# Left-operand sums of the down projection formed once and kept in DRAM, the sample tile first in the output projection, the gate in the accumulation, output rows in two parts

## The chip, the cores and the metric

The kernel runs on one core of a Trainium2 chip. The metric is device time in microseconds (us) of one execution. The engines are named as the profile names them: PE (matrix products; PEld is its weight load), DVE (the vector engine), ACT (the scalar engine), POOL (GpSimd) and SP, whose queue issues every DMA of this kernel in order.

## The reference

One layer of a hybrid encoder for 2048 prompt frames and 32 sample frames, width 1024, in float32. Cut to what matters here:

```
proj = (rmsnorm(x, ln1_g) * (1 + sc1) + sh1) @ w_in       # q, k, v for attention, u for the state-space layer
attn = sliding_window_attention(q, k, v)                  # 512 columns
ssm  = gelu_and_glu(state_space(u))                       # 512 columns
x    = x + g1 * (concat(rmsnorm(attn), rmsnorm(ssm)) @ w_out)
h2   = rmsnorm(x, ln2_g) * (1 + sc2) + sh2
ff   = (silu(h2 @ w_gate) * (h2 @ w_up)) @ w_down         # 1024 -> 2816 -> 1024
y    = x + g2 * ff
```

The modulation vectors sh1, sc1, g1, sh2, sc2, g2 come from the conditioning vector, one set for the prompt and one for the sample.

## The kernel before, in words

There are four stages. Stage A projects the 16 prompt tiles of 128 frames and the sample tile (number 16, `NPT`) and writes q, k, v and u to DRAM. Stage B runs the state-space layer with part of the attention. Stage C runs the rest of the attention, the GLU (`c_prep`, units in the order `UNITS`), the norms (`c_norm`) and the output projection (`c_out`), the last two tile by tile in the order `TILES`: 8 to 15, 0 to 7, then the sample tile. Stage F is the feed-forward part. The stages overlap: each is written as Python generators ("flows") that are advanced in turn, and a scheduler at compile time orders the instructions of each engine by the program's order, letting later ones pass when earlier ones aren't ready in its own simulation. On the chip each engine's order is then fixed.

Every product is made from two float32r parts of each operand: `split` (L111) copies the high part on ACT and subtracts it on DVE for the low part, and three matmuls (high by high, high by low, low by high) are accumulated.

**Stage F** works on three panels of frames (`PIECES`, 704, 704 and 672 columns; half of a panel, `w`, is 352, 352 and 336). In a panel, layer 0 multiplies by `w_gate` and `w_up` (11 units of 256 columns each), and layers 1 to 3 multiply by row blocks of `w_down` (2 units each; 1024, 1024 and 768 rows). A unit is a Strassen-Winograd scheme: seven products (`PRODUCTS`, L68, p = 0 to 6) in place of eight, each for two weight blocks (m = 0, 1), so 24 matmuls of `w` columns for each m and k group of four, and 18 in layer 3. One product is called a step. The left operands are the weight quarters 11, 12, 21, 22 and four sums of them, s1 to s4. The right operands are the four quarters of the panel and four sums, t1 to t4.

- `start_unit` (L1526), called one unit ahead, loads four half blocks [128, 4, 256] through `weights` (six buffers `wr`).
- `prepare` (L1531), called three steps ahead (`AHEAD`), forms the sums on POOL in place: s1 and s3 at p = 0, s2 at p = 1, s4 at p = 2, 128x512 elements each, for both m, and then splits the operand of its step (`wh` on ACT, `wl` on DVE). This happens in all four layers and in all three panels, so that the sums of `w_down`, which are the same each time, are formed three times.
- `prepare_right` (L1560), six steps ahead and in the first unit of a layer only, splits the seven right operands (`bh`, `bl`, 128x1408) and forms t1 to t4 with four subtractions on DVE (`q`).
- `finish` (L1648) takes the results from PSUM. In layer 0 it makes silu(gate) * up (`finish_in`), whose last product runs on POOL, and stores it to `f_d`. In layers 1 to 3 `finish_out` (L1631) adds to the accumulators `acc`, with part of the additions on POOL (`c<-c,acc`).
- `out_rows` (L1585) is started after the last product of each half of layer 3: it multiplies the four accumulators by g2 on ACT, and for each of six pieces loads the rows of x (`xr`, three buffers), transposes (`fo`), adds on DVE and stores.
- `h_steps` (L1419) makes the next panel's right operand while layer 3 runs (transposes `ft`).

Of the kernel before, what the change touches and what calls it, by code (L numbers as in the profile page):

```python
# [50 lines left out]
LATE = [0, 1, 2, 3, 4, 5]  # L51
TILES = [*range(8, NPT), *range(8), NPT]
UNITS = [4, 5, 6, 7, 0, 1, 2, 3, 8]
BLOCKS = [2, 0, 1, 3]
PSB = 5
# [17 lines left out]
def hybrid_kernel(  # L73
# [1021 lines left out]
    def attention_tile(j):  # L1095
# [21 lines left out]
        if j < NPT:  # L1117
            vcur = kv_split(kf, vf, kt[:, :, 128:256], n)
            if j == TILES[0]:
# [163 lines left out]
    def c_prep(u):  # L1283
# [39 lines left out]
        ssm[u] = (mh, ml, ss)  # L1323
        if h:
            g_load({2: 3, 3: 0, 0: 1, 1: 4}[b])
        yield 1
# [34 lines left out]
    def c_out(j):  # L1361
# [5 lines left out]
        c0 = 128 * (j % 2)  # L1367
        if j in (TILES[0], NPT):
            g1b[0] = pcw.tile([128, D], F32, tag="g1b", name="g1b", bufs=1)[0:n]
            SP.dma_start(g1b[0], gr_d[s:s + 1].to_broadcast([n, D]))  # L1370
# [48 lines left out]
    def h_steps(sb):  # L1419
# [3 lines left out]
        for grp in (PIECES[sb][0:3], PIECES[sb][3:6]):  # L1423
# [23 lines left out]
            col = c  # L1447

    cg = wo_steps(range(4, 8), stage, 512)
    fp = Flow(c_prep, 9, 1, 0)  # L1450
# [38 lines left out]

    class Layer:  # L1490
        def __init__(self, sb, i):
            self.sb, self.i, self.w = sb, i, HALF[sb]
            self.kt = 3 if i == 3 else 4
            self.units = KF // 2 if i == 0 else 2

        def weights(self, u, m):

            kt = self.kt
            out = []
            for h in range(2):  # L1500
                r = pwr.tile([128, 4, 256], F32, tag="wr", name="wr", bufs=6)[:, 0:kt]
                if self.i == 0:
                    src = (w_gate, w_up)[m][0, h * 512:(h + 1) * 512, u * 256:(u + 1) * 256]
                else:
                    row = (self.i - 1) * 1024 + h * kt * 128
                    src = w_down[0, row:row + kt * 128, (2 * u + m) * 256:(2 * u + m + 1) * 256]
                SP.dma_start(r, src.rearrange("(k p) n -> p k n", p=128))
                out.append(r)
            return out

        def load(self):

            q = quads(self.kt)
            qd[self.sb, self.i] = q
            for a in range(2):
                m = 8 * (self.i - 1) + a * self.kt
                for b in range(2):
                    SP.dma_start(q[a][b][:, :, 0:self.w],
                                 f_d[self.sb][m:m + self.kt, :, b * self.w:(b + 1) * self.w].rearrange("k p n -> p k n"))

    layers = [Layer(sb, i) for sb in range(3) for i in range(4)]
    steps = [(L, u, p) for L in layers for u in range(L.units) for p in range(7)]
    raw, left, right = {}, {}, {}
    acc = {}

    def start_unit(n):  # L1526
        if n < len(steps):
            L, u, _ = steps[n]
            raw[L, u] = [L.weights(u, m) for m in range(2)]

    def prepare(n):  # L1531

        if n >= len(steps):
            return
        L, u, p = steps[n]
        kt, w = L.kt, L.w
        an, bn, _ = PRODUCTS[p]
        qs = []
        for m in range(2):
            r0, r1 = raw[L, u][m][0:2]  # L1540
            a11, a21, a12, a22 = r0[:, :, 0:128], r0[:, :, 128:256], r1[:, :, 0:128], r1[:, :, 128:256]
            if p == 0:
                s1 = pwr.tile([128, 4, 128], F32, tag="s1", name="s1", bufs=2)[:, 0:kt]
                raw[L, u][m].append(s1)
                tt(P, s1, a21, a22, ADD)
                tt(P, a21, a11, a21, SUB)
            elif p == 1:
                tt(P, a11, raw[L, u][m][2], a11, SUB)
            elif p == 2:
                tt(P, a12, a12, a11, SUB)  # L1550
            qs.append({"11": a11, "12": a12, "22": a22, "s1": raw[L, u][m][2], "s2": a11, "s3": a21, "s4": a12}[an])
        left[n] = []
        for m in range(2):
            h, l = (pv.tile([128, 4, 128], F32R, tag="wv", name=nm, bufs=4 * AHEAD + 4)[:, 0:kt] for nm in ("wh", "wl"))
            split(h, l, qs[m], A, V)
            left[n].append((h, l))
        if u == L.units - 1 and p == 6:
            raw.pop((L, u))

    def prepare_right(n):  # L1560
# [24 lines left out]
    def out_rows(L, half):  # L1585

        sb = L.sb
        ns = sum(n for j, _, n in PIECES[sb] if j < NPT)
# [5 lines left out]
        col = 0  # L1594
        tiles = [acc.pop(d) for d in range(4 * half, 4 * half + 4)]
        for j, r0, n in PIECES[sb]:
            hs_ = slice(half * 512, (half + 1) * 512)
            row = j * 128 + r0
            xr = pwr.tile([128, 512], F32, tag="xr", name="xr", bufs=3)[0:n]
            SP.dma_start(xr, x1_d[row:row + n, hs_])  # L1600
            pb = fp_["t"].tile([128, 512], F32, tag="ft", name="fo")[0:n]
# [3 lines left out]
            SP.dma_start((y_sample[0] if j >= NPT else y_prompt[0, row:row + n])[:, hs_], xr)  # L1605
            col += n
            yield 1
# [23 lines left out]
    def finish_out(L, u, m, qd_, c, bank):  # L1631
        w = L.w
        i, j = qd_
        d = 4 * u + 2 * m + i
        if L.i == 1 and d not in acc:
            acc[d] = pv.tile([128, 2 * HW], F32, tag=f"acc{d}", name="acc")
        o = acc[d][:, j * w:(j + 1) * w]
        if c is None:
            if L.i == 1:
                act(o, bank)  # L1640
            else:
                tt(V, o, bank, o, ADD)
        else:
            if L.i > 1:
                tt(P, c, c, o, ADD)
            tt(V, o, bank, c, ADD)

    def finish(n):  # L1648
        L, u, p = steps[n]
        w = L.w  # L1650
        for m in range(2):
            x, y, z = (banks.get((t, m)) for t in "xyz")
            if p in (0, 2, 4):
                c = keep()[:, 0:w]
                act(c, x[:, 0:w])
                cs[m, p] = c
            if p in (1, 4, 5, 6):
# [7 lines left out]
    start_unit(0)  # L1665
    for n in range(6):
        if n < AHEAD:
            prepare(n)
        prepare_right(n)
    coming = []  # L1670
    for n, (L, u, p) in enumerate(steps):
        li = layers.index(L)
# [81 lines left out]
```

## Time and profile before

| | |
|---|---|
| three runs | 2426.49, 2432.91, 2432.59 us; median 2432.59 |
| the profiled execution's own time | 2427.46 us |
| its span, first to last instruction | 2425.6 us |
| mean granted TensorE clock | 0.961 |
| DVE, ACT, POOL busy, share of the span | 73%, 52%, 58% |
| stage F, from about 954 us on | 1472 us |

A row of the view of windows gives, for a stretch of the span, the busy time and the count of instructions of each engine, the granted clock and the share of the DMA engines. A row of a group gives the line, the engine, what is written from what, the shape, the count, and then busy time and mean. The chain of waits gives start, duration and what ran, along the chain of work that ended last. Names such as `wl`, `bl`, `q` are the program's tile names.

### The profile page before, as it was taken

What the parts mean: (1) busy time and instruction counts of PE and PEld (TensorE: products, weight loads), DVE (VectorE), ACT (ScalarE), POOL (GpSimd) and SP (SyncE); (2) the same over time, 40 slices, a digit from 0 to 9 for tenths busy, and PEclk for the clock granted to TensorE, in tenths of its full rate; (3) what the DMA queues carried; (4) which work ended last, traced back from release to release, by engine and by line L of the source; (5) the groups of instructions that cost most, each with busy time, mean ns of one, the idle gap of its engine ahead of it and who ended that gap; (6) DMA issues with size and microseconds to landing.
All of it is one profiled execution on the core that took longest, in us unless ns stands there. A gap on an engine that the chain in (4) does not pass through costs nothing.

```text
span 2425.6 us, 38219 instructions
## 1 busy us (share of the span) xinstructions
PE 2238.5 (92%) x13262; PEld 2068.3 (85%) x13262; DVE 1769.5 (73%) x2722; ACT 1264.8 (52%) x2557; POOL 1418.6 (58%) x1277
## 2 busy tenths in 40 slices
PE   7888998997998898899999999999999989999987
PEld 4677777886887786799999888999989889999887
DVE  6878876778687754855568988655589896667995
ACT  5645435546555555444445575444455754445543
POOL 1177766784655645655555665655556646555563
PEclk8898998998999999899999999999999999999999
DMA  7757767764221223333324335333243254332322
GB/s 232 263 174 211 229 204 230 226 212 156 83 74 56 69 76 132 112 125 124 110 99 130 97 122 185 119 124 111 98 129 97 81 171 144 124 127 96 124 91 92
DMA packets 291455, 331.03 MB, mean 136 GB/s; under 512 B 50798, under 2 KB 237258, under 8 KB 291260
## 3 DMA queue, kind: packets, MB, share of 16 engines
q1 hardware_dynamic: 291260, 328.58, 43.2%
q8 instruction: 104, 1.70, 0.3%
q14 instruction: 91, 0.75, 0.1%
HBM read 247.14 MB, written 81.37 MB: 135 GB/s over the span
## 4 chain that ended last, share of the span: by engine, by line
PE 58%; DVE 11%; DMA 5%; POOL 4%; issue 4%; ACT 3%; SPq 0%; DVEq 0%; ACTq 0%; POOLq 0%
PE fx L116 25%; PE fy L116 12%; PE fz L116 6%; PE co L116 4%; DVE wl L88 3%; DVE bl L88 2%; PE cb L116 2%; PE ob L116 1%; DVE q L88 1%; PE y L116 1%; DMA wr<-in_w_down_dram 1%; POOL wr L88 1%; PE qp L116 1%; PE pt L1067 1%; DMA out_dram<-xr 1%
## 5 line engine op out<-in xcount | busy, mean ns | idle before, releaser
L88 DVE TENSOR_TENSOR wl<-wr,wh 128x512 fp32r<-128x512 f32 (+1 forms) x612 | 567.9, 941 | 253.3 <-ACT wh L100 240.3
L100 ACT ACTIVATE wh<-wr 128x512 fp32r<-128x512 f32 (+1 forms) x612 | 374.7, 617 | 550.0 <-PE fx L116 298.1
L116 PE MATMUL fx<-bh,wh 128*128 128x352 f32 (+1 forms) x1584 | 514.4, 325 | 16.5 <-ACT wh L100 7.1
L116 PE MATMUL fx<-bl,wh 128*128 128x352 f32 (+1 forms) x1584 | 512.3, 323 | 9.5 <-DVE bl L88 9.5
L116 PE MATMUL fx<-bh,wl 128*128 128x352 f32 (+1 forms) x1584 | 513.6, 324 | 1.8 <-DVE wl L88 1.8
L88 POOL TENSOR_TENSOR s<-wr 128x512 f32<-128x512 f32 (+1 forms) x102 | 145.4, 1426 | 365.4 <-DVE wl L88 180.6
L88 POOL TENSOR_TENSOR wr<-wr 128x512 f32<-128x512 f32 (+1 forms) x204 | 325.7, 1599 | 43.7 <-DVE wl L88 38.8
L116 PEld LDWEIGHTS fx<-bh,wh 128*128 128x128 f32 x1584 | 302.3, 191 | 19.9 <-ACT wh L100 8.0
L116 PEld LDWEIGHTS fx<-bl,wh 128*128 128x128 f32 x1584 | 303.1, 191 | 10.3 <-DVE bl L88 10.3
L116 PEld LDWEIGHTS fx<-bh,wl 128*128 128x128 f32 x1584 | 301.8, 191 | 3.0 <-DVE wl L88 2.7
L116 PE MATMUL fy<-bh,wh 128*128 128x352 f32 (+1 forms) x792 | 256.2, 324 | 15.1 <-DVE acc L88 13.1
L116 PE MATMUL fy<-bh,wl 128*128 128x352 f32 (+1 forms) x792 | 254.6, 322 | 2.3 <-DVE wl L88 2.3
L116 PE MATMUL fy<-bl,wh 128*128 128x352 f32 (+1 forms) x792 | 254.4, 321 | 0.0
L88 POOL TENSOR_TENSOR wr<-s,wr 128x512 f32<-128x512 f32 (+1 forms) x102 | 152.2, 1500 | 83.0 <-DVE wl L88 82.9
L88 POOL TENSOR_TENSOR c<-c 128x352 f32<-128x352 f32 (+1 forms) x99 | 136.5, 1378 | 83.7 <-ACT wh L100 56.4
L88 DVE TENSOR_TENSOR bl<-q,bh 128x1408 fp32r<-128x1408 f32 (+3 forms) x84 | 164.0, 1957 | 5.3 <-ACT bh L100 5.2
L116 PEld LDWEIGHTS fy<-bh,wh 128*128 128x128 f32 x792 | 150.0, 189 | 19.7 <-DVE acc L88 16.5
L100 ACT ACTIVATE c<-fx 128x352 f32<-128x352 f32 (+1 forms) x339 | 150.3, 444 | 4.9 <-PE fx L116 4.8
L116 PEld LDWEIGHTS fy<-bh,wl 128*128 128x128 f32 x792 | 149.0, 188 | 3.2 <-DVE wl L88 3.2
L116 PEld LDWEIGHTS fy<-bl,wh 128*128 128x128 f32 x792 | 149.9, 189 | 0.0
L116 PE MATMUL fz<-bh,wh 128*128 128x352 f32 (+1 forms) x396 | 129.1, 326 | 15.0 <-ACT wh L100 15.0
L100 ACT ACTIVATE bh<-q 128x1408 fp32r<-128x1408 f32 (+3 forms) x84 | 107.4, 1284 | 65.1 <-DVE q L88 64.8
(386 smaller groups left out, 5435.9 us busy)
## 6 DMA issues: line engine op xcount, KB each, us to landing
wr<-in_w_gate_dram SPq DMA_DIRECT2D x66, 512.0 KB
wr<-in_w_up_dram SPq DMA_DIRECT2D x66, 512.0 KB
wr<-in_w_down_dram SPq DMA_DIRECT2D x48, 512.0 KB
adw<-in_w_ada_dram SPq DMA_DIRECT2D x64, 256.0 KB
f_d<-c SPq DMA_DIRECT2D x88, 176.0 KB
sm<-sm_d SPq DMA_DIRECT2D x32, 448.0 KB
q<-f_d SPq DMA_DIRECT2D x16, 704.0 KB
wr<-in_w_down_dram SPq DMA_DIRECT2D x24, 384.0 KB
```

The lines of the kernel that those rows point to most:

```text
L88: e.tensor_tensor(out, a, b, op=op)
L100: A.activation(out, a, func, **kw)
L116: PE.matmul(out, lhsT, rhs, start=start, stop=stop, skip_group_check=more)
L1067: PE.transpose(pt[:, kb, i * 128:(i + 1) * 128], pbuf[:, kv * npair + i, kb * 128:kb * 128 + 128], ident)
```

## The change

- **Sums once.** In the first panel's layer 0, from its second unit on, a new generator `down_sums` loads the quarters of the twelve `w_down` blocks, forms their four sums on POOL and stores them to DRAM (`sd_d`). In layers 1 to 3 `load_left` loads the operand of each step directly, a quarter of `w_down` or a sum from `sd_d`, nine steps ahead (`FAR`). `prepare` then only splits.
- **Weight tiles.** All weight loads are now quarters [128, 4, 128], in 13 buffers of a pool that opens before stage F, so that the first unit's loads and its first sums are issued inside stage C. `start_unit` forms s1 and s3 right after its loads.
- **t3 and t2** (the second and third of the four subtractions) move from DVE to POOL.
- **Sample first.** `TILES` and `UNITS` put the sample tile and its unit first, in attention, GLU, norm and output projection; the loads of the GLU's input and of g1 follow that order.
- **Gate in the accumulation.** The products are multiplied by g2 as they leave PSUM (ACT's copy with a scale, DVE's `scalar_tensor_tensor`), and `out_rows` no longer multiplies.
- **Rows in two parts.** `out_rows` is started for pieces 0 and 1 after p = 5 and for pieces 2 to 5 after p = 6, with the rows of x of all its pieces loaded first into six buffers.

```
-TILES = [*range(8, NPT), *range(8), NPT]
-UNITS = [4, 5, 6, 7, 0, 1, 2, 3, 8]
+TILES = [NPT, *range(8, NPT), *range(8)]
+UNITS = [8, 4, 5, 6, 7, 0, 1, 2, 3]
+FAR = 9
+XR = 6
...
+    sd_d = dram.tile([12, 4, 128, 512], F32, name="sd_d")
...
+    def wtile(kt):
+        return fp_["q"].tile([128, 4, 128], F32, tag="wr", name="wr", bufs=13)[:, 0:kt]
+    def start_unit(n):
+        if n < len(steps) and steps[n][0].i == 0:
+            L, u, _ = steps[n]
+            raw[L, u] = [{t: quarter(L, u, m, t, wtile(4)) for t in ("21", "22", "11", "12")} for m in range(2)]
+            for r in raw[L, u]:
+                r["s1"] = wtile(4)
+                tt(P, r["s1"], r["21"], r["22"], ADD)
+                tt(P, r["21"], r["11"], r["21"], SUB)
+                r["s3"] = r["21"]
+    def load_left(n):
+        if n < len(steps) and steps[n][0].i:
+            L, u, p = steps[n]
+            t = PRODUCTS[p][0]
+            for m in range(2):
+                x = wtile(L.kt)
+                if t in WHERE:
+                    quarter(L, u, m, t, x)
+                else:
+                    SP.dma_start(x.rearrange("p k n -> p (k n)"),
+                                 sd_d[(L.i - 1) * 4 + 2 * u + m, int(t[1]) - 1, :, 0:L.kt * 128])
+                raw[n, m] = x
+    def down_sums():
+        for L in layers[1:4]:
+            for u in range(2):
+                for m in range(2):
+                    r = {t: quarter(L, u, m, t, pv.tile([128, 2 * HW], F32, tag=f"acc{i}", name="dq")[
+                        :, 0:L.kt * 128].rearrange("p (k n) -> p k n", n=128)) for i, t in enumerate(WHERE)}
...
+                    yield 1
+                    for i, (o, x, y, op) in enumerate(((s1, r["21"], r["22"], ADD), (r["21"], r["11"], r["21"], SUB),
+                                                       (r["11"], s1, r["11"], SUB), (r["12"], r["12"], r["11"], SUB))):
+                        tt(P, o, x, y, op)
+                        SP.dma_start(sd_d[(L.i - 1) * 4 + 2 * u + m, (0, 2, 1, 3)[i], :, 0:L.kt * 128],
+                                     o.rearrange("p k n -> p (k n)"))
+                        yield 1
...
-        fq.step(min(fa.done(), 2 * fp.done(), fc.done() + 2))
+        fq.step(min(fa.done(), 2 * fp.done() - 1, fc.done() + 2))
...
-            elif fc.done() >= 6:
+            elif fc.done() >= 7:
+                if (layers[0], 0) not in raw:
+                    start_unit(0)
                 advance(hg[0])
...
-            tt(V, b12, b22, b12, SUB)
+            tt(P, b12, b22, b12, SUB)
...
-            tt(V, b11, b22, b11, SUB)
+            tt(P, b11, b22, b11, SUB)
...
-        for d in range(4 * half, 4 * half + 4):
-            for s, c0, c1 in ((0, 0, ns), (1, ns, 2 * L.w)):
-                if c1 > c0:
-                    act(acc[d][:, c0:c1], acc[d][:, c0:c1], scale=g2c[:, d, s:s + 1])
...
+                stt(o[:, x], bank[:, x], g2c[:, d, s:s + 1], (o if c is None else c)[:, x], MULT, ADD)
...
-        if p == 6 and L.i == 3:
-            live.append(out_rows(L, u))
+        if p > 4 and L.i == 3:
+            live.append(out_rows(L, u, range(0, 2) if p == 5 else range(2, 6)))
...
+        if li == 0 and u:
+            advance(sums, 1 + (n % 4 == 0))
+        load_left(n + FAR)
```

More of the change, by code (lines that the diff above doesn't have):

```diff
@@ L1447, in h_steps, with __init__, block, load @@
             col = c
+    class Layer:
+        def __init__(self, sb, i):
+            self.sb, self.i, self.w = sb, i, HALF[sb]
+            self.kt = 3 if i == 3 else 4
+            self.units = KF // 2 if i == 0 else 2
+        def block(self, u, m):
+            if self.i == 0:
+                return (w_gate, w_up)[m][0, :, u * 256:(u + 1) * 256]
+            c = (2 * u + m) * 256
+            return w_down[0, (self.i - 1) * 1024:(self.i - 1) * 1024 + self.kt * 256, c:c + 256]
+        def load(self):
+            q = quads(self.kt)
+            qd[self.sb, self.i] = q
+            for a in range(2):
+                m = 8 * (self.i - 1) + a * self.kt
+                for b in range(2):
+                    SP.dma_start(q[a][b][:, :, 0:self.w],
+                                 f_d[self.sb][m:m + self.kt, :, b * self.w:(b + 1) * self.w].rearrange("k p n -> p k n"))
@@ new lines, in hybrid_kernel, with quarter @@
+    layers = [Layer(sb, i) for sb in range(3) for i in range(4)]
+    steps = [(L, u, p) for L in layers for u in range(L.units) for p in range(7)]
+    raw, left, right = {}, {}, {}
+    acc = {}
+    WHERE = {"11": (0, 0), "21": (0, 1), "12": (1, 0), "22": (1, 1)}
+    def quarter(L, u, m, name, t):
+        a, b = WHERE[name]
+        SP.dma_start(t, L.block(u, m)[a * L.kt * 128:(a + 1) * L.kt * 128, b * 128:(b + 1) * 128].rearrange(
+            "(k p) n -> p k n", p=128))
+        return t
@@ L1488, in hybrid_kernel @@
     fs1 = ctx.enter_context(tc.tile_pool(name="fs1", bufs=1, space=bass.MemoryType.PSUM, reuse_waits="tile", side="right"))
[L1490 to L1529, printed above, removed]
     def prepare(n):
@@ L1535, in prepare @@
         L, u, p = steps[n]
[L1536 to L1551, printed above, removed]
+        if L.i == 0:
+            qs = []
+            for r in raw[L, u]:
+                if p == 1:
+                    tt(P, r["11"], r["s1"], r["11"], SUB)
+                    r["s2"] = r["11"]
+                elif p == 2:
+                    tt(P, r["12"], r["12"], r["s2"], SUB)
+                    r["s4"] = r["12"]
+                qs.append(r[PRODUCTS[p][0]])
+        else:
+            qs = [raw.pop((n, m)) for m in range(2)]
         left[n] = []
-        for m in range(2):
-            h, l = (pv.tile([128, 4, 128], F32R, tag="wv", name=nm, bufs=4 * AHEAD + 4)[:, 0:kt] for nm in ("wh", "wl"))
-            split(h, l, qs[m], A, V)
+        for x in qs:
+            h, l = (pv.tile([128, 4, 128], F32R, tag="wv", name=nm, bufs=4 * AHEAD + 4)[:, 0:L.kt] for nm in ("wh", "wl"))
+            split(h, l, x, A, V)
             left[n].append((h, l))
-        if u == L.units - 1 and p == 6:
+        if L.i == 0 and p == 6:
             raw.pop((L, u))
@@ L1583, in prepare_right, with out_rows @@
             parts(p, {2: b11, 4: b12, 5: b21, 6: b22}[p])
-    def out_rows(L, half):
-        sb = L.sb
-        ns = sum(n for j, _, n in PIECES[sb] if j < NPT)
-        for d in range(4 * half, 4 * half + 4):
-            for s, c0, c1 in ((0, 0, ns), (1, ns, 2 * L.w)):
-                if c1 > c0:
-                    act(acc[d][:, c0:c1], acc[d][:, c0:c1], scale=g2c[:, d, s:s + 1])
+    def out_rows(L, half, pieces):
+        hs_ = slice(half * 512, (half + 1) * 512)
+        tiles = [acc[d] for d in range(4 * half, 4 * half + 4)]
+        xs = []
+        for j, r0, n in [PIECES[L.sb][i] for i in pieces]:
+            xr = pwr.tile([128, 512], F32, tag="xr", name="xr", bufs=XR)[0:n]
+            SP.dma_start(xr, x1_d[j * 128 + r0:j * 128 + r0 + n, hs_])
+            xs.append(xr)
         yield 1
[L1594 to L1597, printed above, removed]
+        for i, xr in zip(pieces, xs):
+            j, r0, n = PIECES[L.sb][i]
+            col = sum(x[2] for x in PIECES[L.sb][:i])
             row = j * 128 + r0
-            xr = pwr.tile([128, 512], F32, tag="xr", name="xr", bufs=3)[0:n]
-            SP.dma_start(xr, x1_d[row:row + n, hs_])
             pb = fp_["t"].tile([128, 512], F32, tag="ft", name="fo")[0:n]
@@ L1654, in finish @@
                 c = keep()[:, 0:w]
-                act(c, x[:, 0:w])
+                if L.i == 0:
+                    act(c, x[:, 0:w])
+                else:
+                    i, j = {0: (0, 0), 2: (0, 1), 4: (1, 1)}[p]
+                    d = 4 * u + 2 * m + i
+                    for s, cols_ in columns(L, j):
+                        act(c[:, cols_], x[:, cols_], scale=g2c[:, d, s:s + 1])
                 cs[m, p] = c
@@ L1661, in finish @@
                 (finish_out if L.i else finish_in)(L, u, m, qd_, c, bank)
-        if p == 6 and L.i == 3:
-            live.append(out_rows(L, u))
-    start_unit(0)
+        if p > 4 and L.i == 3:
+            live.append(out_rows(L, u, range(0, 2) if p == 5 else range(2, 6)))
+    if (layers[0], 0) not in raw:
+        start_unit(0)
     for n in range(6):
+        prepare_right(n)
         if n < AHEAD:
             prepare(n)
-        prepare_right(n)
     coming = []
+    sums = down_sums()
     for n, (L, u, p) in enumerate(steps):
```

33 lines of the change are left out of this document (16 added, 17 removed).

## The prediction, made before the changed kernel ran

> **What bounds the kernel now.** I read the stages first, in the view of windows, with the stretches cut where a panel's layers begin (the columns are named in the first row).
>
> ```profile
> PE 2238.5 (92%) x13262; PEld 2068.3 (85%) x13262; DVE 1769.5 (73%) x2722; ACT 1264.8 (52%) x2557; POOL 1418.6 (58%) x1277
> core 0: us, PE busy (x) PEld busy (x) DVE busy (x) ACT busy (x) POOL busy (x), PEclk, DMA share, GB/s
> 953.50:1015.30 61.80, 40.38 (x197) 35.43 (x196) 52.60 (x47) 32.88 (x52) 40.03 (x26) 0.81 0.42 136
> 1015.30:1284.90 269.60, 268.59 (x1674) 268.30 (x1673) 158.88 (x212) 128.32 (x242) 150.72 (x109) 1.00 0.36 116
> 1284.90:1472.00 187.10, 169.01 (x1025) 164.36 (x1024) 161.83 (x173) 112.93 (x191) 114.85 (x75) 0.98 0.37 115
> 1499.50:1769.70 270.20, 269.19 (x1681) 268.88 (x1679) 163.00 (x216) 128.38 (x242) 153.09 (x109) 1.00 0.38 121
> 1769.70:1961.40 191.70, 173.93 (x1045) 168.05 (x1043) 165.26 (x173) 115.06 (x201) 112.29 (x75) 0.97 0.33 101
> 1987.10:2244.70 257.60, 256.01 (x1671) 255.71 (x1670) 180.98 (x215) 128.60 (x243) 150.96 (x108) 1.00 0.40 128
> 2244.70:2411.40 166.70, 151.71 (x961) 147.33 (x959) 141.85 (x162) 82.46 (x149) 95.22 (x67) 0.99 0.31 97
> 2411.40:2425.60 14.20, 4.32 (x25) 2.52 (x24) 4.46 (x7) 1.89 (x5) 0.00 (x0) 0.76 0.53 177
> ```
>
> Layer 0 of each panel (second, fourth and sixth stretch) is bound by PE, idle for about 1 us in 269.6. Nothing is to be won there, only to be lost. Layers 1 to 3 (third, fifth, seventh) are not: PE is idle for 18.1, 17.8 and 15.0 us, while DVE is busy for 85% or more. The start of stage F (first row: 21.4 us idle at a clock of 0.81) and the tail (last row) are the other two losses.
>
> PE's floor follows from the chain of waits, which in layer 0 is PE step after step; the next rows are p = 2 and p = 3 of a unit, p = 2 nine units later, p = 2 in the third panel, and three transposes.
>
> ```profile
> 1023.00 3.87 PE fx L116 x24
> 1026.87 3.87 PE fy L116 x24
> 1265.64 3.87 PE fx L116 x24
> 1994.49 3.68 PE fx L116 x24
> 903.55 0.33 PE ft L1435 x3
> ```
>
> A unit takes (1265.64 - 1023.00) / 9 = 26.96 us, a step 3.85. Layers 1 to 3 have 28 steps of 24 matmuls and 14 of 18: 28 x 3.85 + 14 x 2.89 = 148.3 us, in the third panel 28 x 3.68 + 14 x 2.76 = 141.7. Their transposes (48 `ft` and 48 `fo`, 0.11 us each) add 10.6, in the third panel 2.6 for 24 `fo` before the last product. The floors are 158.9, 158.9 and 144.3 us against 187.1, 191.7 and 166.7: at most 28, 33 and 22 us can be won.
>
> Why is PE idle there? The timeline of DVE and POOL shows it, in rows of engine, operation, shape and count:
>
> ```profile
> 968.89 1.96 POOL L88 TENSOR_TENSOR s<-wr 128x512 f32<-128x512 f32 x1 [4.08 <-DMA wr<-in_w_gate_dram]
> 969.65 2.68 DVE L88 TENSOR_TENSOR bl<-q,bh 128x1408 fp32r<-128x1408 f32 x1
> 970.93 2.53 POOL L88 TENSOR_TENSOR wr<-wr 128x512 f32<-128x512 f32 x1
> 972.26 3.43 DVE L88 TENSOR_TENSOR wl<-wr,wh 128x512 fp32r<-128x512 f32 x2
> ```
>
> POOL's sum ends at 970.85 and DVE's split, begun in its middle, ends 1.48 us later; POOL's next, begun behind it, ends 1.13 us after that split. The two take turns: while one of them reads two operands from SBUF, the other stands still, though both count as busy. Undisturbed durations are the shortest and middle ones of the rows by tile (min/median/max in ns; layers 1 to 3 of the first panel; the 384- and 1056-wide forms are layer 3's):
>
> ```profile
> L88 DVE TENSOR_TENSOR wl<-wr,wh x62: 541/683/1781, 1288.8 to 1433.4; 128x512 fp32r<-128x512 f32 x44, 128x384 fp32r<-128x384 f32 x18
> L88 DVE TENSOR_TENSOR q<-q,q x10: 1242/1612/2008, 1284.6 to 1404.6; 128x1408 f32<-128x1408 f32 x6, 128x1056 f32<-128x1056 f32 x4
> L88 POOL TENSOR_TENSOR s<-wr x10: 1010/1298/2568, 1295.4 to 1423.3; 128x512 f32<-128x512 f32 x6, 128x384 f32<-128x384 f32 x4
> L88 POOL TENSOR_TENSOR c<-c,acc x18: 943/1278/2333, 1355.6 to 1431.1; 128x352 f32<-128x352 f32 x18
> L88 DVE TENSOR_TENSOR acc<-fy,c x18: 510/512/525, 1310.1 to 1432.8; 128x352 f32<-128x352 f32 x18
> ```
>
> The last one reads PSUM and is never lengthened; the others are. Counts, from the groups of 1284 to 1472 us:
>
> ```profile
> L88 DVE TENSOR_TENSOR wl<-wr,wh 128x512 fp32r<-128x512 f32 (+1 forms) x75 | 68.6, 940 | 10.2 <-ACT wh L100 10.0
> L88 DVE TENSOR_TENSOR wl<-s,wh 128x512 fp32r<-128x512 f32 (+1 forms) x12 | 11.9, 992 | 1.2 <-ACT wh L100 1.2
> L88 DVE TENSOR_TENSOR bl<-q,bh 128x1408 fp32r<-128x1408 f32 (+1 forms) x22 | 43.3, 1968 | 2.1 <-ACT bh L100 2.1
> L88 DVE TENSOR_TENSOR q<-q,q 128x1408 f32<-128x1408 f32 (+1 forms) x13 | 23.5, 1816 | 0.0
> L88 POOL TENSOR_TENSOR wr<-wr 128x512 f32<-128x512 f32 (+1 forms) x26 | 44.0, 1695 | 4.3 <-DVE wl L88 3.5
> L88 POOL TENSOR_TENSOR wr<-s,wr 128x512 f32<-128x512 f32 (+1 forms) x12 | 18.1, 1518 | 11.2 <-DVE wl L88 11.2
> L88 POOL TENSOR_TENSOR s<-wr 128x512 f32<-128x512 f32 (+1 forms) x12 | 18.1, 1506 | 47.0 <-DVE wl L88 26.9 <-DMA wr<-in_w_down_dram 9.7 <-DVE q L88 7.1
> L88 POOL TENSOR_TENSOR c<-c,acc 128x352 f32<-128x352 f32 x24 | 32.6, 1371 | 3.8 <-ACT c L100 3.8
> ```
>
> With a third of the weight and right-operand work at layer 3's size, the undisturbed sum is 58 x 0.683 + 29 x 0.541 for `wl`, 24 x 1.612 + 11 x 1.242 for `bl` and `q` together, 33 x 1.298 + 17 x 1.010 for the 50 sums and 24 x 0.943 for `c`: 190.3 us of work that can't overlap, in 187.1 us (102%; starts overlap a little). This shared access of DVE and POOL bounds layers 1 to 3. In layer 0 the same count is 140 `wl`, 80 sums and 30 products `c` in ten units: 95.6 + 103.8 + 28.3 = 227.7 in 269.6 us, 84%, and PE stays full.
>
> **The change part by part.** The sum is made against the profiled execution's 2427.46 us (span 2425.6).
>
> *Sums gone from layers 1 to 3.* Of the 50, some 8 belong to the next panel's first unit; 42 go: 26 x 1.298 + 16 x 1.010 = 50 us. The two subtractions moved take 6.5 x 1.5 = 10 us from DVE and put them on POOL, where no row is so wide: the step from 352 to 512 elements (0.943 to 1.298) is 2.2 ns an element, so about 3.3 us at 1408 and 2.5 at 1056, by proportion up to 3.8, and not under DVE's 1.61; I take 20 us in all. The sum is 190.3 - 50 - 10 + 20 = 150 us against a floor of 158.9, 95%, above layer 0's 84%. So PE becomes the bound, not quite full: the last unit of a layer still holds all seven splits for the next. I take half of the way from the floor for what stays uneven: 168, 170 and 152 us, so **-19, -22 and -15**. At best the floor; at worst nothing. The loads take the place of POOL's work: two quarters a step, nine steps (35 us) ahead, at a DMA share of about a third before.
>
> *Sums formed in the first panel's layer 0.* 48 more on POOL, 32 x 1.298 + 16 x 1.010 = 57.7 us: 227.7 + 57.7 = 285 in 269.6. At the 102% that layers 1 to 3 reached, it needs 280, +11; if the 48 steps (185 us) that hold them give nothing back later, 156 + 57.7 - 188 = +26. I take **+20**; the low end is 0, if the order puts them where nobody waits. Queued behind them on POOL are s2 and s4 of the gate and up weights, for which ACT's `wh` waits, and on SP, behind a store that waits for its sum, the next unit's weight loads and `f_d` stores; both have three steps (11.6 us) or more.
>
> *Start of stage F.* ACT begins the first right operand at 963.64, 10 us after the last output product, because memory comes free only with the sample tile's serial tail; DVE is then busy without a break past 1000.
>
> ```profile
> 963.42 3.92 DMA wr<-in_w_gate_dram
> 963.64 3.89 ACT L100 ACTIVATE bh<-q 128x1408 fp32r<-128x1408 f32 x3
> ```
>
> With tile 7 last, the tail is one half's chain, some 5 us; the weight load (3.92) and four sums (5.2) are done in stage C. I take **-10** (0 to -25: DVE's splits don't get fewer).
>
> *Sample first.* Its projection and output products move into the idle stretch behind stage B; for that the first full unit's input loads later, and attention begins with the tile that stage A writes last. I take **+3** (-8 to +10).
>
> *Tail.* Of 14.2 us, ACT's scaling and the reload of `xr` behind a store are on the chain:
>
> ```profile
> 2409.87 2.27 ACT acc L100 x3
> 2414.92 2.31 DMA out_dram<-xr
> 2417.24 3.74 DMA xr<-x_d
> ```
>
> With rows loaded before and no scaling, four pieces at about 0.7 us on DVE, a store and its landing (2.3) stay: about 8, **-6** (-2 to -9). The gate on DVE's accumulations costs nothing that counts, since they read PSUM.
>
> Sum: -19 - 22 - 15 + 20 - 10 + 3 - 6 = -49, so 2378.5 for the profiled execution. It lay 5.1 below the median of the three runs, inside their spread; I add half: **2381 us**.
>
> **The rivals.** *B, better (2334):* the sums of layer 0 hide (-20) and layers 1 to 3 reach the floor (-9, -11, -8). For it: PE is full in layer 0 at 84%, and DVE waits for ACT there. Against: 95% and 106% are above all that PE has been full at.
>
> *C, the moved subtractions starve DVE at each layer's change (2418):* eleven changes, two subtractions of 3.3 us, each locking out the split that is next, 73 us, less the 35 that DVE saves: +37. It decides if they fall on the splits that PE needs next. For it: the last unit of a layer is already the dense one. The Trainium skill (Perfetto Trace Analysis, Optimizing Scalar/DVE Operations) warns that DVE and GPSIMD share an SBUF read port, so that moving work between them might not help. The alternating rows above agree; by that rule the move itself is worth nothing or less.
>
> *D, slower (2445):* in the first panel's layer 0 a block of sums is a chain on SP and POOL: loads (3.9), four sums each taking turns with a split (7.9), a store (2.3), 14.1 us, beside 15.4 us for its four steps. SP issues in order; if PE waits for half of each chain, it is 12 x 7 = 84 us in place of the 20, +64. It decides above some 6 us a block, when the gain is gone. Against: weight loads are issued seven steps ahead, and the compile-time order may pass them.
>
> *E, no change (2437):* quarters wait for one of the 13 buffers, or land late, and layers 1 to 3 idle as before, now for DMA: the 56 us don't come. Against: 35 us of lead.
>
> **How the numbers follow.** Chances: forecast 0.52 (2362 to 2400), B 0.15, C 0.15, E 0.10, D 0.08. About 0.3% (7 us) is what can be told from no change: faster 0.82, same 0.10 (E), slower 0.08 (D). The range goes from B's figure to short of E's: 2334 to 2430.
>
> **What would show it.** In the changed profile: no `s<-wr` rows in layers 1 to 3, `wl` there near 0.7 to 0.8 us on average, PE's idle there under 10 us a panel; POOL above 70% busy in the first panel's layer 0 and the stage 10 to 26 us longer; the other two layers 0 as long as before; `q` rows on POOL at 2.5 to 3.8 us; under 9 us from the last product to the end. I am wrong if layers 1 to 3 keep 15 us of idle PE (C or E, by whether PE waits for `bl` or for a DMA), or if the first layer 0 grows by more than 40 (D).

## The result, and the profile after

The changed kernel is slower by 0.6%: 2444.19 us against 2431.18 (medians of six runs each), a ratio of 1.0059 with an interval of 1.0042 to 1.0076. The forecast was 2381. One of the four runs of e3 (below) took 6441.88 us, the others 2486 to 2493, and e3's figures are given without it. The profiled execution took 2443.45 us, span 2441.7, against 2427.46 and 2425.6.

Both traces were cut at the last store of the rows of x (`x_d<-xc`, the end of stage C), at the first product of the first panel's unit 1, and at the first product of each layer 1, by the count of products in PE's order (us; a stretch "layers 1 to 3" runs to unit 1 of the next panel, the last one to the end of the span):

| stretch | before | after | difference |
|---|---|---|---|
| to the last store of x | 963.0 | 1014.5 | +51.5 |
| from there to unit 1 | 52.2 | 58.3 | +6.1 |
| panel 1: units 1 to 10 of layer 0 | 270.9 | 283.3 | +12.4 |
| panel 1: layers 1 to 3, next unit 0 | 212.9 | 199.1 | -13.8 |
| panel 2: units 1 to 10 | 272.0 | 270.7 | -1.3 |
| panel 2: layers 1 to 3, next unit 0 | 215.6 | 200.8 | -14.8 |
| panel 3: units 1 to 10 | 259.9 | 258.4 | -1.5 |
| panel 3: layers 1 to 3 and the end | 179.2 | 156.5 | -22.7 |

The differences add up to 15.9, the span's 16.1 but for rounding. Behind unit 1 the feed-forward part gained 41.7 us, of the kind that was forecast. Stage C lost more than that.

First the feed-forward stretches of the changed kernel, in the view of windows (columns as in the prediction): the start of stage F, then layer 0 and layers 1 to 3 of the first and of the second panel, and the tail.

```profile
1014.80:1072.80 58.00, 37.80 (x168) 35.53 (x169) 51.47 (x36) 26.04 (x40) 51.28 (x28) 0.74 0.56 168
1072.80:1356.10 283.30, 273.41 (x1682) 270.86 (x1681) 190.62 (x213) 128.66 (x246) 206.23 (x143) 0.99 0.58 177
1356.10:1514.80 158.70, 155.74 (x973) 154.33 (x972) 130.89 (x156) 101.79 (x172) 59.24 (x38) 0.99 0.57 174
1825.90:1987.20 161.30, 157.78 (x976) 154.70 (x975) 132.96 (x157) 101.79 (x180) 59.59 (x37) 0.99 0.53 159
2434.10:2441.70 7.60, 2.63 (x18) 1.57 (x16) 4.43 (x8) 0.00 (x0) 0.00 (x0) 1.00 0.50 181
```

The rows that the prediction shows for layers 1 to 3 run on into unit 0 of the next panel (in the first panel to 1472.0 us, while that unit's first product, by the count, is at 1460.8). Cut like the rows above, the first panel's row of the kernel before is

```profile
1286.10:1460.90 174.80, 159.78 (x972) 155.69 (x972) 149.53 (x162) 102.47 (x179) 110.65 (x74) 0.98 0.37 117
```

In layers 1 to 3 PE is now idle for 3.0 us in the first panel and 3.5 in the second, where by this cut it was 15.0 and 12.1; POOL's busy time in the first panel has fallen from 111 to 59 us. The tail is 7.6 us instead of 14.2. In the first row, which should have gained, POOL is busy for 51 of 58 us. Now stage C: one row of the kernel before, then the changed kernel, whole and in four stretches cut at stores.

```profile
563.00:963.50 400.50, 366.03 (x2162) 317.77 (x2162) 275.44 (x458) 224.41 (x585) 221.23 (x199) 0.93 0.29 90
```

```profile
563.00:1014.80 451.80, 383.78 (x2214) 333.55 (x2214) 266.25 (x471) 231.29 (x607) 223.46 (x204) 0.90 0.26 81
691.70:722.20 30.50, 30.50 (x191) 26.99 (x190) 17.09 (x33) 14.81 (x45) 14.94 (x15) 1.00 0.19 65
722.20:747.80 25.60, 15.99 (x94) 14.29 (x93) 18.50 (x32) 12.62 (x36) 12.16 (x12) 0.80 0.11 36
747.80:775.30 27.50, 27.50 (x169) 24.30 (x168) 13.72 (x28) 13.87 (x42) 14.65 (x15) 1.00 0.20 72
775.30:804.50 29.20, 20.18 (x132) 18.45 (x131) 21.08 (x37) 14.59 (x40) 14.44 (x14) 0.82 0.27 68
```

Nearly the same work stands in 451.8 us instead of 400.5; PE's idle time is 68 us instead of 34, and its busy time longer at the lower clock. The stretches show the pattern: full for some 28 us, then starved for some 27. The stores on SP's queue follow it:

```profile
691.74 0.33 SPq L1400 DMA_DIRECT2D x_d<-xc  x1
701.97 0.32 SPq L1400 DMA_DIRECT2D x_d<-xc  x1
710.50 0.32 SPq L1400 DMA_DIRECT2D x_d<-xc  x1
722.22 0.32 SPq L1400 DMA_DIRECT2D x_d<-xc  x1
747.84 0.32 SPq L1400 DMA_DIRECT2D x_d<-xc  x1
```

Four stores (two tiles, one unit), then a gap of 25.6 us. What PE waits for in stage C is named by the waits:

```profile
PE pt L1069 <- POOL pbuf L89: 25.5, 5, 8.2
PE cb L1281 <- DMA gn<-gs_d: 7.1, 1, 7.1
```

The longest entry is a step of attention. It leads astray, as e1 will show: attention is a serial chain, and waits for it show where nothing else is there to run. What is missing is the next unit's GLU products and, for want of them, its output products: of the GLU's `cb` matmuls 36 run in 691.7 to 722.2 us and 12 in 722.2 to 747.8, of the output's `co` 78 and 20.

**Theory T1.** The order of the flows sets a limit that the change left as it was: `fp.step(fc.done() // 2 + 2)`, where `fc.done()` counts the tiles that the output projection has finished. It lets the GLU of unit m start when `fc.done() // 2 + 2` exceeds m. With full units first, unit m holds tiles 2m and 2m+1, and it may start with two tiles before it still to come. With the one-tile sample unit first, unit m holds tiles 2m-1 and 2m, and the same limit lets it start with one tile to come. **Rivals:** T2, the sample tile in stage B pushes a full attention tile into stage C; T3, only the first full unit is late; T4, the early loads and sums of the first feed-forward unit disturb stage C.

### The profile page after: what moved, and what is told of

It is laid out like the page before. It is cut to its first block, busy times and chain, and to the rows that moved or that the text cites. A ratio compares the mean times of both kernels' runs of the same rounds, so it can differ in the third digit from the quotient of the medians.

```text
span 2441.7 us, 39053 instructions
## 1 busy us (share of the span) xinstructions
PE 2236.6 (92%) x13262; PEld 2071.0 (85%) x13262; DVE 1771.0 (73%) x2722; ACT 1259.8 (52%) x2547; POOL 1341.2 (55%) x1205
## 4 chain that ended last, share of the span: by engine, by line
PE 47%; DVE 4%; DMA 2%; issue 1%; POOL 1%; ACT 0%; SPq 0%; DVEq 0%; POOLq 0%; ACTq 0%
PE fx L117 27%; PE fy L117 13%; PE fz L117 6%; DVE wl L89 2%; DVE bl L89 1%; DMA wr<-in_w_up_dram 1%; POOL dq L89 1%; DMA dq<-in_w_down_dram 1%; PE fo L1640 0%; DVE q L89 0%; POOL c L89 0%; DMA xf<-x_d 0%; PE ft L1437 0%; POOL wr L89 0%; DVE xr L89 0%
## 5 line engine op out<-in xcount | busy, mean ns | idle before, releaser
L89 DVE TENSOR_TENSOR wl<-wr,wh 128x512 fp32r<-128x512 f32 (+1 forms) x714 | 722.9, 1030 | 241.8 <-ACT wh L101 237.7
L101 ACT ACTIVATE wh<-wr 128x512 fp32r<-128x512 f32 (+1 forms) x714 | 434.1, 616 | 561.5 <-PE fx L117 303.2
L89 POOL TENSOR_TENSOR wr<-wr 128x512 f32<-128x512 f32 x264 | 394.3, 1503 | 162.2 <-DVE wl L89 145.3
L89 POOL TENSOR_TENSOR c<-c 128x352 f32<-128x352 f32 (+1 forms) x99 | 146.5, 1481 | 166.2 <-ACT wh L101 107.6
L89 POOL TENSOR_TENSOR c<-c,acc 128x352 f32<-128x352 f32 (+1 forms) x72 | 84.3, 1175 | 173.2 <-ACT c L101 169.7
L89 POOL TENSOR_TENSOR q<-q,q 128x1408 f32<-128x1408 f32 (+3 forms) x24 | 87.8, 3661 | 118.9 <-DVE q L89 86.7
L89 DVE TENSOR_TENSOR bl<-q,bh 128x1408 fp32r<-128x1408 f32 (+3 forms) x84 | 148.8, 1773 | 5.6 <-ACT bh L101 5.6
L101 ACT ACTIVATE bh<-q 128x1408 fp32r<-128x1408 f32 (+3 forms) x84 | 107.7, 1284 | 51.5 <-DVE q L89 28.2
L117 PE MATMUL fz<-bh,wl 128*128 128x352 f32 (+1 forms) x396 | 129.5, 327 | 2.3 <-DVE wl L89 2.2
```

The source lines that it names most:

```text
L89: e.tensor_tensor(out, a, b, op=op)
L101: A.activation(out, a, func, **kw)
L117: PE.matmul(out, lhsT, rhs, start=start, stop=stop, skip_group_check=more)
```

## The experiments

Each is compared with the kernel before on the same chip (ratio and its interval). e1 to e4 ran on one chip, e5 to e8 on a second, e9 to e12 on a third, e13 and e14 on a fourth; between these groups the ratios are the better measure.

| kernel | median, us | ratio to before |
|---|---|---|
| e1_ahead | 2404.83 | 0.9906 (0.9883 to 0.9928) |
| e2_order_back | 2394.70 | 0.9861 (0.9846 to 0.9875) |
| e3_order_alone | 2489.60 | 1.0253 (1.0236 to 1.0270) |
| e4_t23_dve | 2387.25 | 0.9839 (0.9819 to 0.9859) |
| e5_ahead_less | 2481.83 | 1.0204 (1.0189 to 1.0220) |
| e6_order_t23 | 2375.21 | 0.9772 (0.9749 to 0.9794) |
| e7_sums_back | 2403.49 | 0.9875 (0.9855 to 0.9895) |
| e8_no_sums | 2353.19 | 0.9675 (0.9661 to 0.9690) |
| e9_pool_beside | 2412.11 | 0.9922 (0.9891 to 0.9952) |
| e10_rows_one_part | 2373.33 | 0.9769 (0.9749 to 0.9790) |
| e11_sums_later | 2376.61 | 0.9790 (0.9759 to 0.9821) |
| e12_sums_burst | 2401.53 | 0.9890 (0.9869 to 0.9911) |
| e13_sums_after_u0 | 2365.86 | 0.9721 (0.9692 to 0.9750) |
| e14_before_7wr | 2422.22 | 0.9937 (0.9908 to 0.9966) |

### Stage C: the order or its look-ahead

e1, the changed kernel:

```
-        fp.step(fc.done() // 2 + 2)
+        fp.step((fc.done() + 1) // 2 + 2)
```

> The changed kernel with one line altered: the normalisation of unit m of the gated scan output (the products cb) may start when (tiles out + 1) // 2 + 2 > m, rather than tiles out // 2 + 2 > m, which with the one-tile sample unit first gives back the two tiles of look-ahead that the kernel before had. Theory T1 (look-ahead of the output projection halved by the order): the pairs of stores with gaps of 25 to 32 us go, stage C shrinks from 457 us to 400 to 415, the first product of unit 1 comes at 1015 to 1030 us, the total is 2390 to 2405 us. Rival T2 (the sample tile in the scan stage pushes a full attention tile into stage C, and the attention chain sets its length): 2435 to 2445, gaps stay. Rival T3 (only the first full unit comes late, behind the sample's gate round trip): a gain of at most 20 us, 2425 to 2440. Rival T4 (loads and sums of the first feed-forward unit, issued inside stage C, disturb it): 2435 to 2445.

e5, the kernel before, order unchanged:

```
-        fp.step(fc.done() // 2 + 2)
+        fp.step((fc.done() - 1) // 2 + 2)
```

> The kernel before, its order of tiles unchanged (sample last), with one line altered so that unit m of the gated scan output may start only when one tile of the unit before is left, not two: (tiles out - 1) // 2 + 2. It is the look-ahead of the changed kernel without its order. T1 (the look-ahead is what costs): stage C 30 to 55 us longer, stores in pairs with gaps of 25 us and more, total 2458 to 2485 us. Rival (the order itself costs, the look-ahead little): within 15 us of before, 2428 to 2443.

e3 takes `TILES`, `UNITS` and the limits of the change into the kernel before, and nothing else:

> The kernel before with the new order of tiles alone (sample tile first, with the limits that the change gave it). T1, T2 and T3: stage C is 45 to 60 us longer than before, total 2475 to 2495 us against 2431. T4: within 10 us of before, 2425 to 2440. My blind forecast had the order at +3, with -10 from an earlier first unit: 2424 to 2440.

e2 takes them out of the changed kernel:

> The changed kernel with the order of tiles alone put back (sample tile last, its limits with it); the feed-forward changes stay. T1, T2 and T3 all put the loss on the order: the first product of unit 1 comes at 1005 to 1020 us, total 2385 to 2400 us; it is also the feed-forward's own gain, which the traces put at 41 us (2390). T4 (early loads in stage C): 2430 to 2445, the loss stays.

The rows of the stores of x give the end of stage C (first and last start, us) in the changed kernel, e1, e5, e3 and e2:

```profile
L1400 SPq DMA_DIRECT2D x_d<-xc x34: 318/320/339, 611.1 to 1014.5; - x34
```

```profile
L1400 SPq DMA_DIRECT2D x_d<-xc x34: 319/320/424, 613.1 to 970.1; - x34
```

```profile
L1398 SPq DMA_DIRECT2D x_d<-xc x34: 302/320/337, 617.1 to 1012.0; - x34
```

```profile
L1398 SPq DMA_DIRECT2D x_d<-xc x34: 318/320/382, 616.0 to 1018.8; - x34
```

```profile
L1400 SPq DMA_DIRECT2D x_d<-xc x34: 318/320/423, 616.5 to 965.8; - x34
```

One line gives back 44.4 of the 51.5 us (e1). The wait for attention falls with it, from 25.5 us to 8.1 (10.9 in the kernel before), though nothing of attention was changed:

```profile
PE pt L1069 <- POOL pbuf L89: 8.1, 3, 4.2
```

The new order alone, in the kernel before, costs 55.8 us of stage C (e3). In the kernel before, the shorter look-ahead alone, with the order untouched, costs 49 us of stage C and 2% of the time (e5), and its stores fall into the same pattern:

```profile
721.57 0.32 SPq L1398 DMA_DIRECT2D x_d<-xc  x1
729.50 0.32 SPq L1398 DMA_DIRECT2D x_d<-xc  x1
740.11 0.32 SPq L1398 DMA_DIRECT2D x_d<-xc  x1
750.98 0.32 SPq L1398 DMA_DIRECT2D x_d<-xc  x1
780.56 0.33 SPq L1398 DMA_DIRECT2D x_d<-xc  x1
```

T1 holds. T2 and T3 fall with e1 and e5, T4 with e2, e3 and e5. The order itself, at equal look-ahead, still costs a little: by the medians e1 is 10 us above e2, and e4 (below) 12 above e6 (16 by the ratios, since these two ran on different chips); in both pairs only the order differs. The profiled executions of e1 and e2 lie only 3.8 us apart. In e1 stage C ends 4.3 us later than in e2, and the first feed-forward product then follows 8.8 us behind the last store of x, in e2 2.6. e1's chain of waits goes through a load of rows there:

```profile
966.91 0.63 ACT q L101
...
967.58 1.07 PE ft L1437 x6
...
969.35 6.47 DMA xf<-x_d
...
975.90 1.15 ACT xf L101
```

These rows aren't needed yet. The first panel's two groups of rows, with 24 transposes each, are through at 968.4 us; the three loads at 968.45 to 969.35 are the first group of the second panel (only six of its 24 transposes run before unit 0, the other 18 near 1438). The compile-time order has put their scaling (`xf` on ACT) ahead of the first `bh` of unit 0, so ACT waits for them. In e2 the same three loads start at 955.75 to 956.61 and are there in time. The changed kernel has e1's order and waits 2.6 us only, so this is no fixed price of the order; why the first panel's rows come so late in e1 stays open.

### The subtractions t2 and t3 on POOL (rival C)

e4, on e1 (e6 is the same edit on e2):

```
-            tt(P, b12, b22, b12, SUB)
+            tt(V, b12, b22, b12, SUB)
...
-            tt(P, b11, b22, b11, SUB)
+            tt(V, b11, b22, b11, SUB)
```

> As e1, and the two subtractions of the right factors (t2 and t3, 128x1408 each) on DVE again, as before the change; it is read against e1. My view (the two engines take turns in layers 1 to 3, so it matters little where the work is): within 8 us of e1, either way, and the loss, if any, in layers 1 to 3. Rival C (on POOL they hold DVE off, so the move cost time): e4 faster than e1 by 10 us or more. Rival (POOL was free, DVE is the bound at panel changes): e4 slower than e1 by 10 us or more.

> Sample tile last as before and the subtractions t2 and t3 on DVE as before; the sums of the down weights, the gate scale in the accumulation and the rows in two parts stay. If the two effects add (order back 2394.7, t2 and t3 back -17.6): 2375 to 2382 us. If they overlap: 2385 to 2395.

The move had cost 17.6 us (e4 against e1), and without the new order 19.5 by the medians or 22 by the ratios (e6 against e2, on different chips): rival C was right in kind, and the effects add. It shows at the change to the third panel, in the timeline of DVE and POOL; first e1, then e4.

```profile
1941.43 7.07 POOL L89 TENSOR_TENSOR q<-q,q 128x1344 f32<-128x1344 f32 x2
1943.04 6.01 DVE L89 TENSOR_TENSOR wl<-wr,wh 128x512 fp32r<-128x512 f32 x2
```

```profile
1937.24 3.52 DVE L89 TENSOR_TENSOR q<-q,q 128x1344 f32<-128x1344 f32 x2
1942.38 1.57 DVE L89 TENSOR_TENSOR wl<-wr,wh 128x512 fp32r<-128x512 f32 x2
```

While POOL makes the two subtractions, two splits on DVE take 6.01 us instead of 1.57. In the whole changed kernel 22 splits `wl` take more than 2 us (2.3 to 3.7), each beside another one of the 24 subtractions moved; in e4 and e6 none does (longest 1.82). Together the four instructions need 5.1 us on DVE alone; beside each other they hold both engines for 7.6. The Trainium skill (Perfetto Trace Analysis, Optimizing Scalar/DVE Operations) says that the two share a read port, so that moving work between them might not help; here the move cost.

e9 asks whether it is the hold or the longer latency. On e6, behind each of the two subtractions:

```
+            zq = pwr.tile([128, 512], F32, tag="xr", name="zq", bufs=XR)
+            for z0 in range(0, L.kt * w, 256):
+                z1 = min(256, L.kt * w - z0)
+                tt(P, zq[:, 0:z1], cpk[:, 0:z1], cpk[:, 0:z1], ADD)
```

> As e6 (t2 and t3 on DVE), and beside each of the 24 subtractions t2 and t3 POOL adds constants into an unused tile, six instructions of together 128x1408, which nothing waits for. It is read against e6, and splits the 17.6 us that t2 and t3 on POOL cost in e4 against e1. Contention (POOL's work holds DVE off, wherever the result goes): 8 to 20 us above e6, DVE's bl and wl longer beside it. Latency (the chain of the right factors waits for POOL's 3.66 us in place of DVE's 1.53): within 5 us of e6.

By the ratios it is 1.5% above e6, some 36 us, with nothing waiting for the results. Latency alone is out. The price is above both expectations, though. The profiled execution, the fastest of e9's four, is 26.7 us longer than that of e6, and 11.7 of them lie in units 1 to 10 of the first panel, where POOL has the sums of the down weights to form as well. Nearly all of these are one wait; the longest wait of PE in the same units of e6 is 6.2:

```profile
PE fx L117 <- DVE wl L89: 10.5, 1, 10.5
```

It is one split. The chain of waits has the split, and the timeline of POOL what ran beside it (in all eleven instructions, one behind the other):

```profile
1030.03 11.24 DVE wl L89
```

```profile
1030.19 1.27 POOL L89 TENSOR_TENSOR wr<-wr 128x512 f32<-128x512 f32 x1
...
1034.66 2.48 POOL L89 TENSOR_TENSOR wr<-wr 128x512 f32<-128x512 f32 x2
...
1040.10 0.61 POOL L89 TENSOR_TENSOR zq<-cpk 128x256 f32<-128x256 f32 x1
```

A 128x512 split that takes 0.68 us alone stands for 11.2 us, and ends 0.6 us after the last of POOL's run; POOL's instructions in it take no longer than they do undisturbed. So here the two don't take turns: DVE is held off for as long as POOL has work without a gap. Why the split didn't get in between, as splits do from 1050 us on, the trace doesn't say. In the second and third panel, where POOL has more room, units 1 to 10 grew by 4.1 and 3.8 us and the third panel's unit 0 by 4.7.

### The sums of the first panel, and the start of stage F

e8, on e6: `tt(P, o, x, y, op)` of `down_sums` is left out, and the stores write raw quarters.

> As e6, with the 48 POOL instructions that form the sums of the down weights in the first layer 0 left out; the loads and the 48 stores stay and store raw quarters (the output is not the reference's). Theory (the 13 us that the first layer 0 grew are POOL's hold on DVE and its queue): units 1 to 10 of the first panel take 270 to 274 us instead of 281, total 8 to 11 us under e6. Rival (the loads and stores in SP's queue make the 13 us): within 3 us of e6.

It saved 22 us, not 8 to 11. Units 1 to 10 gave back 10.1, as the theory had it; but 14 came from unit 0, whose products stand ahead of all the sums in the program. The rows of the windows for unit 0 and units 1 to 10, of e6 and e8:

```profile
963.60:1020.20 56.60, 38.36 (x169) 35.19 (x170) 53.66 (x37) 24.18 (x37) 51.44 (x27) 0.73 0.65 197
1020.20:1303.70 283.50, 274.09 (x1681) 273.23 (x1681) 187.30 (x216) 128.72 (x245) 197.62 (x138) 0.98 0.56 171
```

```profile
965.30:1007.90 42.60, 33.77 (x169) 31.47 (x170) 37.82 (x37) 23.70 (x37) 28.84 (x13) 0.86 0.91 279
1007.90:1281.30 273.40, 271.44 (x1682) 271.15 (x1682) 171.13 (x216) 130.34 (x245) 146.25 (x104) 0.99 0.58 174
```

In unit 0 of e6 POOL has 27 instructions, in e8 13: the scheduler had let the sums pass. DVE, which splits the seven right operands there, is busy for 53.7 of 56.6 us in e6 and for 37.8 in e8, with the same 37 instructions. The timeline of e6 in unit 0 shows one sum after another, and the splits beside them:

```profile
967.96 2.65 POOL L89 TENSOR_TENSOR ds<-dq 128x512 f32<-128x512 f32 x1
970.69 2.53 POOL L89 TENSOR_TENSOR dq<-dq 128x512 f32<-128x512 f32 x1
```

```profile
973.69 2.69 DVE L89 TENSOR_TENSOR q<-q,q 128x1408 f32<-128x1408 f32 x1
977.99 2.70 DVE L89 TENSOR_TENSOR bl<-q,bh 128x1408 fp32r<-128x1408 f32 x1
```

e11 begins the sums one unit later in the program (`if li == 0 and u > 1`):

> As e6 with the sums of the down weights begun one unit later (from unit 2 of the first layer 0 on). In the traces of e6 and e8 POOL ran the first sums already in unit 0, while DVE split the right factors at 2.7 us each instead of 1.6, and unit 0 took 56.6 us with them and 42.6 without. If it is this: unit 0 takes 42 to 45 us, the total is 2360 to 2365 us (e6 2375). Rival (POOL runs ahead again, or the sums cost the same wherever they lie): 2370 to 2378.

Nothing changed (unit 0: 56.7 us): POOL's order came out the same, since a later place in the program holds nothing back that the scheduler finds ready. e13, on e6, makes it a true dependence:

```
+        if n == 6:
+            for i in range(4):
+                late = pv.tile([128, 2 * HW], F32, tag=f"acc{i}", name="late")
+                act(late[:, 0:1], bank[:, 0:1])
```

> As e6, with four one-column ACT copies of unit 0's last product into the buffers that the first sums of the down weights are loaded to, so that their loads, and with them POOL's sums, can't run before unit 0's products are done. (In e11 the later place in the program had changed nothing: the order at compile time had put POOL's sums at the same place, in unit 0.) Theory (the sums that POOL runs during unit 0 hold off DVE's splits of the right factors): unit 0 takes 42 to 46 us instead of 56.6, units 1 to 10 stay at 280 to 286, total 2358 to 2367 us against e6's 2375. Rival (the cost only moves: the sums cost the same later): unit 0 42 to 46 us, units 1 to 10 294 or more, total 2370 to 2378.

The windows of e13, unit 0 and units 1 to 10:

```profile
968.10:1010.70 42.60, 34.38 (x169) 31.53 (x170) 37.85 (x37) 23.95 (x37) 28.84 (x13) 0.85 0.28 82
1010.70:1293.60 282.90, 274.92 (x1682) 272.46 (x1681) 200.32 (x216) 127.27 (x249) 218.60 (x152) 0.99 0.65 198
```

Unit 0 takes 42.6 us with all the sums still formed, and units 1 to 10 are no longer than in e6: the sums were in the way in unit 0, and the cost is not just moved. The DMA share in unit 0 is 0.28 here and 0.91 in e8, for the same 42.6 us, so DMA has no part in it. At 2365.86 us e13 is the fastest version that forms the sums: 2.8% under the kernel before, 3.2% under the change by the medians.

### Layers 1 to 3, and the tail

In e6 the stretches of layers 1 to 3 gained 61.9 us in all (17.4, 24.8 and 25.8, less 6.1 of the tail); some 55 of them lie in these layers and 7 in the next panels' unit 0. e7, on e6, puts POOL's additions back:

```
+            if L.i and PRODUCTS[p][0][0] == "s":
+                tt(P, x, x, x, ADD)
```

> As e6, and ahead of the split of each loaded sum in layers 1 to 3 one POOL addition of its 128x512 (it doubles the sum: the output is not the reference's), the same eight POOL instructions per unit, at the same place, that the kernel before had there. It is read against e6. My forecast's reason (DVE and POOL take turns, and it is these sums that layers 1 to 3 waited for): layers 1 to 3 go back towards 213, 216 and 179 us, total 25 to 45 us above e6. Rival (what gained there is the loading: quarters and earlier loads): at most 10 us above e6.

e12 puts them in the former order, four of them at a unit's first product:

> As e7 (an addition on POOL for each loaded sum of layers 1 to 3, which doubles the sum: the output is not the reference's), with the eight additions of a unit in the order in which the kernel before had them: four at the unit's first product, two each at its second and third. It is read against e6 and e7. If the burst at the unit's start is the rest of what the kernel before lost there: 10 to 30 us above e7 (2413 to 2433). If it is the loading: within 8 us of e7 (2395 to 2411).

Both are 26 to 28 us above e6 by the medians; the stretches of e7 are 7.3, 8.5 and 11.3 us longer, and `wl` takes longer, as these groups of the second panel's layers 1 to 3 show, e6 first:

```profile
L89 DVE TENSOR_TENSOR wl<-wr,wh 128x512 fp32r<-128x512 f32 (+1 forms) x81 | 59.1, 745 | 22.4 <-ACT wh L101 22.4
```

```profile
L89 DVE TENSOR_TENSOR wl<-wr,wh 128x512 fp32r<-128x512 f32 (+1 forms) x82 | 73.4, 925 | 8.1 <-ACT wh L101 8.1
L89 POOL TENSOR_TENSOR wr<-wr 128x512 f32<-128x512 f32 (+1 forms) x46 | 61.5, 1344 | 54.3 <-DMA wr<-sd_d 37.8 <-DVE wl L89 16.1
```

So the sums account for some 27 of the 62 us, and less than that is sure to be the hold on DVE, since e7's additions also stood on POOL waiting for their loads (37.8 us in this row). The burst has no part. For the rest, e14 gives the kernel before more lead in its loads (`name="wr", bufs=7` in place of 6):

> The kernel before with seven buffers of half weight blocks in place of six, so that the third of a unit's four loads can run a unit ahead as well; nothing else. It asks for the part of layers 1 to 3 that e7 and e12 did not give back (putting the sums back there cost 28 us, the kernel before lost 62). If it is the lead of the weight loads: units of layers 1 to 3 that took 30 to 35 us shorten to 28 to 31, total 2400 to 2420 us. Rival (the finishing of the products, or the sums' waits on DVE alone): within 6 us of before.

It gained 0.6%, between the two expectations: the three stretches by 2.6, 5.6 and 2.0 us. About 10 us is the lead of the loads, then; if the parts add, some 25 of the 62 are left open between the finishing of the products, a lead longer than a seventh buffer gives, and the two together.

e10, on e6, starts `out_rows` once for each half, after p = 6, with all six pieces:

> As e6 with the rows of each half put out in one part after the last product, as before. Forecast's view (two parts shorten the end): from the last product to the end 12 to 15 us instead of 8.1, total 3 to 8 us above e6. Rival (the gate scale moved into the accumulation did it): 8 to 9 us, total within 3 us of e6.

The tail is 8.2 us (e6: 8.1) and the time the same: the two parts do nothing that can be seen. What is left for the shorter tail is the rows of x loaded ahead and the missing scaling, which the forecast's working had counted; neither was tried alone.

## Why the prediction was wrong

Two of its steps failed, a third was mis-sized, and one rival came true beside the forecast.

- **"Sample first +3 (-8 to +10)": measured +51.5** (e3, the order alone: +55.8; 44.4 of the 51.5 go with e1's one line). The step looked at which products move where and at which loads come later. It did not look at the limits by which the flows are advanced. The order changed how units and tiles line up, and one limit that counts tiles for units stayed. e1 and e5 show it from both sides. This alone turns the forecast's sign.
- **"Start of stage F -10 (0 to -25)": measured +6.1.** The wait that the step named did go: from the last store of x to the first product it is 2.6 us instead of 5.1. It was smaller than the step had it: the last output product ends at 957.83, 5.8 us and not 10 before the first right operand is begun. And the forecast put the sums' POOL time wholly into units 1 to 10, where the program has them, and noted only that the compile-time order might put them where nobody waits. It put 10 of the 48 into unit 0 (in e6 14: POOL's 27 instructions against 13), where DVE was the bound. With that undone (e13) unit 0 takes 42.6 us against 47.1 before and 55.8 after; from the last store of x on, that is 7 us under the kernel before, so the gain is there. The change had also swapped `prepare` and `prepare_right` in the steps made ahead of unit 0, which no run tried alone.
- **"Sums formed in layer 0 +20 (0 to +26)": +12.4 in units 1 to 10.** Where the step had them, the sums cost about half of what it said: 10.1 us by e8 against e6, 9.5 by e13 against e8. That their whole price in e6, 22 us, comes near 20 is luck, since more than half of it lies in unit 0.
- **"-19, -22 and -15" for layers 1 to 3.** With the next unit 0 it was -13.8 and -14.8, in the third panel -16.1 (-22.7 less 6.6 of the tail), together -44.7 for a forecast of -56. PE became the bound, as the step had it, with 3 us idle and not 9. What stayed is the panel change, which the step's stretches held in part: unit 0 of the second panel went from 38.1 to 40.5 us, that of the third from 40.5 to 39.5. There the moved subtractions stand in the way, and with them on DVE (e6) the last one takes 31.8. The reason behind the step, that DVE and POOL take turns, is borne out where it was tested, but the sums it removed are less than half of what was won (e7, e14).
- **Rival C (2418).** Its mechanism is real: 22 of the 24 subtractions hold off a split each. It was priced at +37 beside the forecast's sum and costs 18.
- **"Tail -6": -6.6.** Right in size. Of the reasons given, the one that only four pieces stay behind the last product had no share: with all six there (e10) the tail is as short.
- **Rival D** fell: the twelve blocks cost 22 us, 1.8 each and not 7. **E** fell as well.

Every sign listed under "what would show it" came true but the mean of `wl` (0.90 us in the second panel, forecast 0.7 to 0.8) and the longest of the subtractions on POOL (4.57 us, median 3.56, forecast 2.5 to 3.8), and the time went the other way: the list held nothing on stage C, because the step there was believed to cost nothing.

## What to carry to other kernels

When an order of tiles changes, go through every limit that turns a count of one thing into a count of another; a waits view that names a serial chain in a stage that was full before can mean that something else is no longer offered. Work put "in a later stage" of the program may be started as early as its operands allow unless a true dependence holds it back: check which engine its own shares an access path with, and what that one does then. And moving an operation of two SBUF operands from DVE to POOL is not free even while POOL is idle; compare how long the neighbours on DVE take beside it.

## What the runs showed of the hardware

The hold between DVE and POOL is close to complete for wide operands: a 128x1408 split takes 1.61 us alone and 2.70 beside POOL's 128x512 sums (e6), which go from 1.28 to 2.5 and more; DVE's instructions that read PSUM stay at 0.51. The Trainium skill (SBUF — State Buffer, Who interferes with whom) says that a DVE instruction with two SBUF inputs contends with a GpSimd instruction that reads SBUF; the rows agree. The two mostly take turns, but not always: in e9 one 128x512 split stood for 11.2 us beside eleven POOL instructions that followed each other without a gap.

PE's granted clock goes with its feeding in stretches of some 25 to 30 us: in stage C of the changed kernel it was 1.00 in the full ones and 0.80 to 0.82 in the starved ones between them. The last 7.6 us of that kernel show 1.00 with PE busy for 2.6 us, so it doesn't in every short stretch.
